# Attention's small matmuls: two places of a half step instead of four

## The chip, the cores and the metric

The kernel runs on one core of a Trainium2 chip. The metric is the device time of one execution in microseconds (us); lower is better. The engines named here are PE (TensorE, matmuls), DVE (VectorE), ACT (ScalarE), POOL (GpSimd) and SP, whose queue starts the transfers. Each engine takes its instructions in the order of the program and meets the others through semaphores.

## The reference, cut to what matters

One layer of an encoder, applied to two requests of 512 tokens each, so 1024 tokens. Cut to the attention branch:

```python
proj = rmsnorm(x) @ w_in                    # 1024 tokens x 1024, into q, k, v of 3 groups x 8 heads x 64
q, k = rope(rmsnorm(q)), rope(rmsnorm(k))   # per head
for g, (window, dilation) in enumerate(((128, 1), (512, 4), (2048, 16))):
    s = q @ k.T * 64 ** -0.5                # within the group's band
    p = exp(s - max(s)); o = p @ v          # sums and maxima are kept, the groups are joined later
```

Around it stand an RG-LRU branch, the output product and a convolutional FFN, which the change does not touch.

## The kernel before

**Stages.** The program runs through the norm and the recurrent branch (to about 410 us), the projections of v, k and q with the attention in between (410 to 975 us), the gate product `GELU(x @ w)` (to about 1080 us), the output product and the FFN. Every large product is split into three matmuls (high x high, high x low, low x high) of 128x512, lines L758 to L760 in the attention stage. I call these three, for one slice `k` of the contraction, a *slice*.

**The attention stage** is a loop over nine column blocks (`ci`: v, k, q of group 0, then of groups 1 and 2) and within it over eight token tiles `t`. One pass is a *step*: eight slices into one accumulator `ps`. A step is cut into two *half steps* of four slices (`hlf` 0 and 1), and between those slices the small matmuls of the attention of earlier tiles are put by hand:

- `slot_qk()` takes two *units* (512 score columns each) and issues their scores into `sp` (L642). On DVE it issues, per unit, mask add (L651), row maximum (L654) and a scaling of it (L656), then the exponentials on ACT (L658), which write `p`. In groups 1 and 2 it acts in every other half step.
- `slot_pt(new)` transposes the `p` of the two units that were scored a half step before: four transposes each into a PSUM tile `pt` (L666), and a copy to `pT` by DVE (L668).
- `slot_pv()` multiplies the transposed pairs with v into `o` (L679); ACT copies a finished `o` out (L682).
- `pend_T()` runs where a normed q or k tile is due (only in half step 0): four transposes of `kn` into a tile `pt` (L606), and a copy to `qkT` by DVE (L608). It also makes new units.

At the end of a q or k step `qk_norm` squares the finished `ps` on ACT (L577) and sums it on DVE (L580). A half step later DVE scales (L586, L588), and another one later it rotates (L595 to L597); the rotated `kn` is what `pend_T` transposes two steps after its product.

**The tile that both kinds of transposes share** has two buffers:

```python
pt = ps2.tile([128, 4, 128], F32, tag="tr", bufs=2, name="pt")   # in to_T (L606) and in emit_pt (L666)
```

A third tile of this tag may be written only when the copy out of the first is done. The other accumulators have three (`proj`), two (`s`) and one (`o`) bank.

**Order around the change.** In a half step: slice, `slot_qk`, slice, `slot_pv`, slice, (in half step 0) `pend_T`, slice, `slot_pt`, `tick`. `tick` lets the deferred scaling or rotation go to DVE. The gate stage goes on with the same slots until the units are used up, eight slices to a half step, with `pend_T` directly ahead of `slot_pt`.

Of the kernel before, what the change touches and what calls it, by code (L numbers as in the profile page):

```python
# [112 lines left out]
def layer_kernel(ctx: ExitStack, tc: tile.TileContext, xs_in, norm1_g, w_in, conv_w, conv_b, lru_wa, lru_ba,  # L113
# [518 lines left out]
    def emit_scores(us):  # L632
        for u in us:
            u.sp = ps2.tile([128, 512], F32, tag="s", bufs=2, name="sp")
        nk = len(us[0].keys)
        for i in range(len(us[0].heads)):
            for j in range(nk):
                c0 = (i * nk + j) * 128
                for u in us:
                    h, kk = u.heads[i], u.keys[j]  # L640
                    p0 = 64 * (h % 2)
                    PE.matmul(out=u.sp[:, c0:c0 + 128], lhsT=u.qT[p0:p0 + 64, h // 2, :],  # L642
                              rhs=kk[0][p0:p0 + 64, h // 2, :], start=True, stop=True)

    def emit_qk(u):
        sp, nh = u.sp, len(u.heads)
        if u.first:
            u.t.num = ap.tile([128, 528], F32, tag="num", bufs=2, name="num")
        h0 = u.heads[0]
        p = ap.tile([128, nh, u.w], F32, tag="p", bufs=4, name="p")  # L650
        V.tensor_tensor(out=p, in0=sp.rearrange("p (h k) -> p h k", h=nh),  # L651
                        in1=u.mask.rearrange("p (o k) -> p o k", o=1).to_broadcast([128, nh, u.w]), op=ALU.add)
        mx = u.t.num[:, 512 + h0:512 + h0 + 2 * nh - 1:2]
        V.tensor_reduce(out=mx, in_=p, axis=AX.X, op=ALU.max)  # L654
        nm = ap.tile([128, nh], F32, tag="nm", bufs=4, name="nm")
        V.tensor_scalar(out=nm, in0=mx, scalar1=-0.125, scalar2=None, op0=ALU.mult)  # L656
        for i in range(nh):
            act(out=p[:, i], in_=p[:, i], func=AF.Exp, scale=0.125, bias=nm[:, i:i + 1],  # L658
                accum_out=u.t.num[:, 520 + h0 + 2 * i:521 + h0 + 2 * i])
        u.p = p  # L660
# [11 lines left out]
    def emit_pv(u):  # L672
        tl = u.t
        if u.first:
            tl.o = ps2.tile([128, 512], F32, tag="o", bufs=1, name="o")
        nk = len(u.keys)
        for i, h in enumerate(u.heads):
            for j, kk in enumerate(u.keys):
                PE.matmul(out=tl.o[:, 64 * h:64 * h + 64], lhsT=u.pT[:, i * nk + j, :], rhs=kk[1][:, 64 * h:64 * h + 64],  # L679
                          start=(j == 0), stop=(j == nk - 1))  # L680
        if u.last:
            A.copy(out=tl.num[:, 0:512], in_=tl.o)  # L682
            dst = num_d[tl.g]
            if tl.g == 0:
                t0 = 64 + 128 * tl.qi
                if tl.qi < 7:
                    SP.dma_start(out=dst[t0:t0 + 128, :], in_=tl.num)
                else:
                    SP.dma_start(out=dst[T - 64:T, :], in_=tl.num[0:64])
                    SP.dma_start(out=dst[0:64, :], in_=tl.num[64:128])  # L690
            else:
                b, a = divmod(tl.qi, 4)
                SP.dma_start(out=dst[S * b:S * b + S, :].rearrange("(j a) c -> a j c", a=4)[a], in_=tl.num)
            ndone[tl.g, tl.qi] = True
# [5 lines left out]
    def slot_qk():  # L700

        turn[0] += 1
        if not units or (units[0].g and turn[0] % 2):
            return []
        new = [units.popleft(), units.popleft()]
        emit_scores(new)
        for u in new:
            emit_qk(u)
        return new

    def slot_pv():
        for u in infl2:
            emit_pv(u)
        infl2.clear()

    def slot_pt(new):
        for u in infl:
            emit_pt(u)
        infl2.extend(infl)
        infl.clear()  # L720
        infl.extend(new)
# [12 lines left out]
    def pend_T():  # L734
        while pend and pend[0][0] <= step[0]:
            _, kn, isq, gg, tt = pend.popleft()
            tT = to_T(kn, isq)
            if not isq:
                kt[gg, tt] = tT
            elif gg == 0:  # L740
                ks = [tt, (tt + 1) % 8]
                add_units(0, tt, tT, [(kt[0, x], vt[0, x]) for x in ks], masks["edge" if tt % 4 == 3 else "band"])
            else:
                add_units(gg, tt, tT, [(kt[gg, tt], vt[gg, tt])], masks[gg])

    for ci in range(9):
        g, typ = ci // 3, "vkq"[ci % 3]
        sl8 = ws.take(8)
        order = [7, 0, 1, 2, 3, 4, 5, 6] if (g == 0 and typ == "q") else list(range(8))
        for t in order:  # L750
            cols = lhs_cols(g, t, typ == "q")
            ps = ps2.tile([128, 512], F32, tag="proj", bufs=3, name="ps")
            ws.adv(1)
            for hlf in range(2):
                for k in range(4 * hlf, 4 * hlf + 4):
                    hi, lo = sl8[k]
                    a, b = xh[:, k, cols], xl[:, k, cols]
                    PE.matmul(out=ps, lhsT=a, rhs=hi, start=(k == 0), stop=False)  # L758
                    PE.matmul(out=ps, lhsT=a, rhs=lo, start=False, stop=False)  # L759
                    PE.matmul(out=ps, lhsT=b, rhs=hi, start=False, stop=(k == KD - 1))  # L760
                    if ci == 8 and t == order[-1]:
                        ws.done("a", 1)
                        ws.adv(1)
                    if k % 4 == 0:
                        new = slot_qk()
                    if k % 4 == 1:
                        slot_pv()
                    if k == 2:
                        pend_T()
                slot_pt(new)  # L770
                tick()
            if typ == "v":
                v_t = ap.tile([128, 512], F32, tag="v", bufs=8, name="v_t")
                A.copy(out=v_t, in_=ps)
                vt[g, t] = v_t
            else:
                if g == 0:
                    ri = (4 if typ == "q" else 0) + t % 4
                else:
                    ri = 8 + t % 4  # L780
                kn = qk_norm(ps, g if typ == "q" else 3 + g, ri, typ == "q")
                pend.append((step[0] + 2, kn, typ == "q", g, t))
            step[0] += 1
        if ci < 8:
            ws.done("ab"[ci % 2], 8)
# [71 lines left out]
    for c in range(KR):  # L857
        if c == ATT_DONE:
            assert not (units or infl or infl2 or pend)
            close(cm_a)  # L860
            cm_y, yp = open_pool("y", side="right")
            cm_o, op_ = open_pool("oT", side="right")
            new_oT()
            for cc in list(held):
                y_split(cc, held.pop(cc))
        slabs = ws.take(2)
        for b in range(2):
            ps = ps2.tile([128, 512], F32, tag="proj", bufs=3, name="ps")
            sl = slice(S * b, S * b + S)
            for ks in (range(1), range(1, 3), range(3, 8)):  # L870
                mm3(ps, wcol(slabs, 0), wcol(slabs, 1), lambda k: xh[:, k, sl], lambda k: xl[:, k, sl], KD, ks)
                if ks[0] == 0:
                    new = slot_qk()
                elif ks[0] == 1:
                    slot_pv()
            if b == 0:
                pend_T()
            slot_pt(new)
            if b == 1:
                ws.done("a", 2)  # L880
                if c + 1 < KR:
                    h_load(c + 1)
                if c >= 2:
                    cg = comb_load(c - 2)
                    defer(3, lambda t=c - 2, cg=cg: combine(t, cg))
            tick()
            ws.adv(1)
            hT = hts.pop((c, b))
            if b == 0 and c < ATT_DONE:
                gl = p3.tile([128, S], F32, tag="yhold", bufs=ATT_DONE, name="yhold")  # L890
            else:
                gl = p3.tile([128, S], F32, tag="gl", bufs=2, name="gl")
            act(out=gl, in_=ps, func=AF.Gelu_apprx_tanh)
            V.tensor_tensor(out=gl, in0=hT, in1=gl, op=ALU.mult)
            if b == 1:
                defer(1, lambda c=c, gl=gl: SP.dma_start(out=y_d[128 * c:128 * c + 128, :], in_=gl))
            elif c < ATT_DONE:
                held[c] = gl
            else:
                y_split(c, gl)  # L900
        step[0] += 1
# [269 lines left out]
```

## Time and profile before

| | |
|---|---|
| time, median of 3 runs | 2167.48 us (2165.16 to 2169.90) |
| the profiled execution | 2167.51 us, its span 2165.7 us |
| PE busy | 2108.1 us, 97% of the span |
| DVE busy | 1072.7 us, 50% |
| ACT busy | 756.6 us, 35% |

PE's busy time contains modelled ends, so it says that PE rarely stands, not that it runs at its peak. What a move of matmuls costs is therefore read from the distance between starts. DVE's mean hides that its share differs by stage.

### The profile page before, as it was taken

Reading aid. Unit: us, or ns where it says so; the run is one execution under the profiler, and the core shown is the slowest. Engines: PE = TensorE matmul, PEld = TensorE weight load, DVE = VectorE, ACT = ScalarE, POOL = GpSimd, SP = SyncE. Lnnn points to the kernel's source line nnn. Section 1 sums busy time; section 2 is a strip of 40 time slices with the busy share of each in tenths; the row PEclk is TensorE's granted clock in tenths of the full one; section 3 lists DMA queues with packets and bytes.
Section 4 is the critical chain, followed back from the end, with each engine's and each line's share of the span. In section 5 each row is a group of like instructions: output and inputs, shape, how many; then the busy total and the mean of one; then the engine's idle time right before and its main releaser. Section 6 shows DMA issues by size and latency. Waiting matters only on the chain. (4 is left out here: it accounts for less than half of the span.)

```text
span 2165.7 us, 25959 instructions
## 1 busy us (share of the span) xinstructions
PE 2108.1 (97%) x9859; PEld 1756.0 (81%) x9859; DVE 1072.7 (50%) x1513; ACT 756.6 (35%) x1269; POOL 771.1 (36%) x658
## 2 busy tenths in 40 slices
PE   7999898999999999999999999999999999999999
PEld 5767676787899999998778888888888888888887
DVE  5499998427862671674654442333233332233324
ACT  4388787412431242145433432411221122212120
POOL 4345656634213422422445444421222222222220
PEclk9999999999999999999999999999999999999999
DMA  4534444411111111104555454211111111111112
GB/s 143 150 95 138 127 124 122 149 48 42 40 41 44 40 55 49 30 28 146 161 197 181 135 159 152 64 49 39 49 49 49 49 44 55 49 49 39 56 41 83
DMA packets 190299, 181.98 MB, mean 84 GB/s; under 512 B 27708, under 2 KB 142942, under 8 KB 190174
## 3 DMA queue, kind: packets, MB, share of 16 engines
q1 hardware_dynamic: 188126, 175.08, 26.6%
q0 software_dynamic: 2048, 5.25, 1.0%
q8 instruction: 78, 1.28, 0.3%
q14 instruction: 47, 0.39, 0.1%
HBM read 141.80 MB, written 33.23 MB: 81 GB/s over the span
## 5 line engine op out<-in xcount | busy, mean ns | idle before, releaser
L228 POOL TENSOR_TENSOR lo<-raw,hi 128x512 fp32r<-128x512 f32 (+1 forms) x384 | 508.8, 1337 | 881.9 <-ACT hi L227 839.1
L150 PE MATMUL ps<-x2h,lo 128*128 128x512 f32 x768 | 301.4, 392 | 0.0
L148 PE MATMUL ps<-x2h,hi 128*128 128x512 f32 x768 | 301.3, 392 | 0.0
L149 PE MATMUL ps<-x2l,hi 128*128 128x512 f32 x768 | 301.2, 392 | 0.0
L227 ACT CAST hi<-raw 128x512 fp32r<-128x512 f32 (+1 forms) x324 | 189.9, 605 | 305.3 <-issue 121.8
L758 PE MATMUL ps<-hi,xh 128*128 128x512 f32 x576 | 251.8, 437 | 0.0
L759 PE MATMUL ps<-lo,xh 128*128 128x512 f32 x576 | 229.1, 398 | 1.7 <-POOL lo L228 1.7
L1094 DVE TENSOR_TENSOR acc<-acc,psd 128x512 f32<-128x512 f32 x192 | 132.0, 687 | 199.3 <-PE psd L1093 199.3
L760 PE MATMUL ps<-hi,xl 128*128 128x512 f32 x576 | 228.6, 397 | 0.0
L148 PE MATMUL ps<-xh,hi 128*128 128x512 f32 x544 | 218.3, 401 | 4.3 <-DVE xc L354 4.3
L150 PE MATMUL ps<-xh,lo 128*128 128x512 f32 x544 | 217.1, 399 | 2.2 <-POOL lo L228 2.2
L149 PE MATMUL ps<-xl,hi 128*128 128x512 f32 x544 | 216.8, 399 | 0.0
L149 PEld LDWEIGHTS ps<-x2l,hi 128*128 128x128 f32 x768 | 144.2, 188 | 32.7
L148 PEld LDWEIGHTS ps<-x2h,hi 128*128 128x128 f32 x768 | 144.2, 188 | 32.5
L150 PEld LDWEIGHTS ps<-x2h,lo 128*128 128x128 f32 x768 | 144.2, 188 | 32.5
L759 PEld LDWEIGHTS ps<-lo,xh 128*128 128x128 f32 x576 | 157.4, 273 | 8.9 <-POOL lo L228 2.6
L758 PEld LDWEIGHTS ps<-hi,xh 128*128 128x128 f32 x576 | 155.2, 270 | 10.5 <-POOL hi L225 0.5
L760 PEld LDWEIGHTS ps<-hi,xl 128*128 128x128 f32 x576 | 155.3, 270 | 8.2
L1091 PE MATMUL psd<-hi,hh 128*128 128x512 f32 x384 | 151.6, 395 | 0.0
L1092 PE MATMUL psd<-lo,hh 128*128 128x512 f32 x384 | 151.5, 395 | 0.0
L1093 PE MATMUL psd<-hi,hl 128*128 128x512 f32 x384 | 151.5, 395 | 0.0
L1049 DVE SCALAR_TENSOR_TENSOR gc<-ps,vff,gc 128x1022 f32<-128x1022 f32 x24 | 30.8, 1281 | 229.2 <-ACT gc L1048 229.2
(188 smaller groups left out, 3540.5 us busy)
## 6 DMA issues: line engine op xcount, KB each, us to landing
raw<-in_w_in_dram SPq DMA_DIRECT2D x144, 256.0 KB
raw<-in_w_up_dram SPq DMA_DIRECT2D x96, 256.0 KB
raw<-in_w_down_dram SPq DMA_DIRECT2D x48, 256.0 KB
sg_d<-sgt SPq DMA_DIRECT2D x16, 512.0 KB
raw<-in_w_lru_out_dram SPq DMA_DIRECT2D x32, 256.0 KB
raw<-in_w_o_dram SPq DMA_DIRECT2D x32, 256.0 KB
cg<-num_d SPq DMA_DIRECT2D x24, 264.0 KB
num_d<-num SPq DMA_DIRECT2D x23, 264.0 KB
```

The source lines that it names most:

```text
L148: PE.matmul(out=ps, lhsT=a, rhs=b, start=(k == 0), stop=False)
L149: PE.matmul(out=ps, lhsT=a, rhs=rl(k), start=False, stop=False)
L150: PE.matmul(out=ps, lhsT=wl(k), rhs=b, start=False, stop=(k == n - 1))
L227: A.copy(out=hi[:, 0:n], in_=r[:, 0:n])
L228: G.tensor_tensor(out=lo[:, 0:n], in0=r[:, 0:n], in1=hi[:, 0:n], op=ALU.subtract)
L758: PE.matmul(out=ps, lhsT=a, rhs=hi, start=(k == 0), stop=False)
L759: PE.matmul(out=ps, lhsT=a, rhs=lo, start=False, stop=False)
L760: PE.matmul(out=ps, lhsT=b, rhs=hi, start=False, stop=(k == KD - 1))
L1091: PE.matmul(out=ps, lhsT=a[0][:, tl], rhs=w[0], start=(i == 0), stop=False)
L1092: PE.matmul(out=ps, lhsT=a[0][:, tl], rhs=w[1], start=False, stop=False)
L1093: PE.matmul(out=ps, lhsT=a[1][:, tl], rhs=w[0], start=False, stop=(i == 1))
L1094: V.tensor_tensor(out=acc[t][:, cl], in0=acc[t][:, cl], in1=ps, op=ALU.add)
```

## The change

The scores and value products of a half step are issued together, ahead of its first slice, value products first. The transposes of `kn` and of `p` are issued together behind the first slice (in the gate stage behind the second), so the remaining slices follow them. The number of instructions on PE and DVE is the same.

```diff
             for hlf in range(2):
+                slot_pv()
+                new = slot_qk()
                 for k in range(4 * hlf, 4 * hlf + 4):
                     hi, lo = sl8[k]
                     a, b = xh[:, k, cols], xl[:, k, cols]
...
                     if ci == 8 and t == order[-1]:
                         ws.done("a", 1)
                         ws.adv(1)
+                    if k == 0:
+                        pend_T()
                     if k % 4 == 0:
-                        new = slot_qk()
-                    if k % 4 == 1:
-                        slot_pv()
-                    if k == 2:
-                        pend_T()
-                slot_pt(new)
+                        slot_pt(new)
                 tick()
...
             ps = ps2.tile([128, 512], F32, tag="proj", bufs=3, name="ps")
             sl = slice(S * b, S * b + S)
-            for ks in (range(1), range(1, 3), range(3, 8)):
+            slot_pv()
+            new = slot_qk()
+            for ks in (range(2), range(2, 8)):
                 mm3(ps, wcol(slabs, 0), wcol(slabs, 1), lambda k: xh[:, k, sl], lambda k: xl[:, k, sl], KD, ks)
                 if ks[0] == 0:
-                    new = slot_qk()
-                elif ks[0] == 1:
-                    slot_pv()
-            if b == 0:
-                pend_T()
-            slot_pt(new)
+                    if b == 0:
+                        pend_T()
+                    slot_pt(new)
```

On PE, in the q steps of group 1, before: from the pending transposes in half step 0 to the value products in half step 1 there is a slice between any two kinds.

```order
L606 MATMUL pt<-ident,kn 128x128 x4
L758 MATMUL ps<-hi,xh 128x512
L759 MATMUL ps<-lo,xh 128x512
L760 MATMUL ps<-hi,xl 128x512
L666 MATMUL pt<-ident,p 128x128 x8
...
L642 MATMUL sp<-qkT 128x128 x8
...
L679 MATMUL o<-v_t,pT 128x64 x8
```

The same place of the changed kernel, where the lines of a slice have moved by two (L760 to L762). Now the eight transposes of `p` follow the four of `kn` at once, and nine large matmuls follow both:

```order
L606 MATMUL pt<-ident,kn 128x128 x4
L666 MATMUL pt<-ident,p 128x128 x8
L760 MATMUL ps<-hi,xh 128x512
...
L679 MATMUL o<-v_t,pT 128x64 x8
L642 MATMUL sp<-qkT 128x128 x8
L760 MATMUL ps<-hi,xh 128x512
```

The scores have moved behind the value products, and both stand ahead of the four slices of the half step.

The same transposes with what they wait for, changed kernel. The rows are the end of the four of `kn`, the four of the first unit and the four of the second:

```order
L606 MATMUL pt<-ident,kn 128x128 x3
L666 MATMUL pt<-ident,p 128x128 [waits PE_49,Activation_49]
L666 MATMUL pt<-ident,p 128x128 [waits Activation_49] x3
L666 MATMUL pt<-ident,p 128x128 [waits DVE_49,Activation_49]
L666 MATMUL pt<-ident,p 128x128 [waits Activation_49] x3
```

The first transpose of the second unit waits for DVE: its tile is the buffer that the pending transposes filled just before.

On DVE the order is the same before and after. In a half step 0 of group 0 it is this, with the copy of the pending transposes (L608) behind the six operations of the scores:

```order
L651 TENSOR_TENSOR p<-sp,msk 128x512
L654 TENSOR_REDUCE num<-p 128x2
L656 TENSOR_SCALAR nm<-num 128x2
L651 TENSOR_TENSOR p<-sp,msk 128x512
L654 TENSOR_REDUCE num<-p 128x2
L656 TENSOR_SCALAR nm<-num 128x2
L608 COPY qkT<-pt 128x512
L668 COPY pT<-pt 128x512 x2
```

Nothing moved in these rows; what moved is when PE wants their results.

## Rows read from the trace of the kernel before

**Rows 1.** The page: busy time, share of the span and instructions of each engine.
```profile
PE 2108.1 (97%) x9859; PEld 1756.0 (81%) x9859; DVE 1072.7 (50%) x1513; ACT 756.6 (35%) x1269; POOL 771.1 (36%) x658
```

**Rows 2.** Busy time by stretch: length, PE, PEld, DVE, ACT, POOL, clock, DMA share, GB/s.
```profile
524.00:646.00 122.00, 119.70 (x889) 105.54 (x888) 93.28 (x177) 47.41 (x154) 25.36 (x24) 1.00 0.13 37
```

**Rows 3.** Timeline of PE, first pair of group 1: start, length, instruction.
```profile
738.49 1.16 PE L642 MATMUL sp<-qkT 64*128 64x128 f32 x16
739.58 0.62 PE L758 MATMUL ps<-hi,xh 128*128 128x512 f32 x1
...
744.07 0.60 PE L606 MATMUL pt<-ident,kn 128*128 128x128 f32 x4
744.42 0.60 PE L758 MATMUL ps<-hi,xh 128*128 128x512 f32 x1
744.86 0.40 PE L759 MATMUL ps<-lo,xh 128*128 128x512 f32 x1
...
745.33 0.60 PE L666 MATMUL pt<-ident,p 128*128 128x128 f32 x4
746.48 0.63 PE L666 MATMUL pt<-ident,p 128*128 128x128 f32 x4 [0.55 <-DVE qkT L608]
746.86 0.60 PE L758 MATMUL ps<-hi,xh 128*128 128x512 f32 x1
```

**Rows 4.** Timeline of PE, the next step of group 1.
```profile
749.88 1.89 PE L679 MATMUL o<-v_t,pT 128*128 128x64 f32 x16
751.58 0.61 PE L758 MATMUL ps<-hi,xh 128*128 128x512 f32 x1
```

**Rows 5.** Timeline of DVE, first pair of group 1.
```profile
739.68 0.69 DVE L651 TENSOR_TENSOR p<-sp,msk 128x512 f32<-128x512 f32 x1
...
743.37 0.29 DVE L597 TENSOR_TENSOR kn<-kn,rt 128x128 f32<-128x128 f32 x1
745.05 0.69 DVE L580 TENSOR_REDUCE ss<-sq 128x8 f32<-128x512 f32 x1 [1.39 <-ACT sq L577]
745.65 0.68 DVE L608 COPY qkT<-pt 128x512 f32<-128x512 f32 x1
```

**Rows 6.** Timeline of ACT, first pair of group 1: last exponential, then the square.
```profile
744.35 0.19 ACT L658 ACTIVATION_READ_ACCUMULATOR p<-p,nm 128x1 f32 x1
744.44 0.57 ACT L577 ACTIVATE sq<-ps 128x512 f32<-128x512 f32 x1
```

**Rows 7.** Timeline of PE, first pair of group 0.
```profile
534.15 0.60 PE L666 MATMUL pt<-ident,p 128*128 128x128 f32 x4
537.05 0.63 PE L666 MATMUL pt<-ident,p 128*128 128x128 f32 x4 [2.30 <-ACT p L658]
537.43 0.48 PE L758 MATMUL ps<-hi,xh 128*128 128x512 f32 x1
537.75 0.39 PE L759 MATMUL ps<-lo,xh 128*128 128x512 f32 x1
537.98 0.40 PE L760 MATMUL ps<-hi,xl 128*128 128x512 f32 x1
```

**Rows 8.** Timeline of all engines, the same place: DVE alone.
```profile
532.96 0.68 DVE L651 TENSOR_TENSOR p<-sp,msk 128x512 f32<-128x512 f32 x1
...
536.22 0.68 DVE L608 COPY qkT<-pt 128x512 f32<-128x512 f32 x1
```

**Rows 9.** Timeline of all engines, gate stage: the transposes of `p`.
```profile
983.52 0.63 PE L666 MATMUL pt<-ident,p 128*128 128x128 f32 x4 [0.86 <-DVE qkT L608]
```

**Rows 10.** Busy time by stretch, columns as in rows 2 (clock third from the end).
```profile
537.90:541.30 3.40, 3.40 (x33) 2.78 (x31) 3.30 (x7) 0.00 (x0) 0.00 (x0) 1.00 0.16 59
...
1139.91:1143.32 3.41, 3.41 (x9) 2.64 (x8) 1.12 (x1) 1.64 (x3) 3.18 (x3) 0.50 0.40 119
1143.32:1146.73 3.41, 3.41 (x16) 2.81 (x15) 1.93 (x3) 0.40 (x1) 0.79 (x2) 1.00 0.89 256
```

**Rows 11.** Timeline of PE, the last wait ahead of the fall in rows 10.
```profile
1138.46 0.47 PE L148 MATMUL ps<-yh,hi 128*128 128x512 f32 x1 [2.37 <-DVE thb L948]
```

## The prediction

> **What bounds the kernel now.** I read four views. The page first: PE is busy for 97% of the span, DVE for half of it [rows 1], so PE's stream of matmuls sets the time, and anything that makes PE stand in the attention stage is paid in full. Then the busy time by stretch, since DVE's half is a mean: while group 0's attention runs, DVE works 93.28 of 122 us [rows 2]. There DVE is nearly as full as PE, and a wait of PE for something at the end of DVE's queue is not short. Third, PE's timeline, read by starts, since the lengths overlap. Last, the timelines of DVE and ACT beside it, to see what the transposes wait for.
>
> **What the change takes away: borders.** It adds and removes no instruction, it moves them. Each return from small to large matmuls costs something: the first large one is followed by the next after 0.44 us where its weights are read strided (744.42 to 744.86) [rows 3], after 0.32 where they are not (537.43 to 537.75), against 0.23 in the stream (537.75 to 537.98) [rows 7]. So a merged border gives back 0.21 in groups 1 and 2 and 0.09 in most of group 0. A group 0 step has seven groups of small matmuls and keeps four (3 x 0.09 = 0.27); a step of groups 1 and 2 has four and keeps two (0.42). Over about 8 steps of group 0, three of them strided, and 16 of the others: 5 x 0.27 + 3 x 0.63 + 16 x 0.42 = 10 us. This is the whole gain in sight, and it is netted below. What the passage from value products to scores costs has no row. From below it is nothing; from above I take another border, 0.09 to 0.21 on some 30 places, 3 to 6 us. I take it near nothing, since both sides are small matmuls, and leave the rest to the range.
>
> **What it adds: a wait in the middle of a half step.** Three tiles of the tag `tr` are now written in a row: pending, first unit, second unit. There are two buffers, so the second unit's four transposes wait until DVE has copied the pending tile (L608). The order shows that wait. Behind it on PE stand the three remaining slices, nine large matmuls, and with them the end of the half step and all that follows. Before the change L608 had a slice and most of a half step more to be done.
>
> *Groups 1 and 2.* The first pair of group 1 shows the whole chain in the kernel before, because it already waits there. Scores start at 738.49, DVE takes them up at 739.68 [rows 3, 5]; the exponentials end at 744.5 and only then ACT squares the finished `ps`, at 744.44 [rows 6]; DVE sums it at 745.05 and copies the pending tile at 745.65 [rows 5]; the second four transposes start at 746.48 [rows 3]. From scores to there it is 7.99 us, and no link of it is a large matmul, so it does not shrink when PE's order changes.
> When will PE want these four? After the change, counted from the start of the scores: 1.09 for the scores (738.49 to 739.58). Then the four slices of half step 1: 18 large ones take 4.49 (739.58 to 744.07), of which the first 0.44, so 0.238 each, and twelve take 3.06. Then one slice of half step 0, 0.71; the pending transposes 0.35 (744.07 to 744.42); the first unit's four, 0.38 (as 746.48 to 746.86) [rows 3]. Together 5.59. The wait is 7.99 - 5.59 = 2.40 us. Less the borders, a step grows by 2.40 - 0.42 = 1.98. Value products (1.70, 749.88 to 751.58) [rows 4] stand before the scores in both counts and drop out.
> The pair of q tile t meets the pending tile of t + 1, and the square is in the chain while q steps last: in group 1 for six pairs, in group 2 for five in the loop (the sixth falls into the gate stage). The first pair of each group waits 0.55 already and merges one border: +1.4. Group 1: 5 x 1.98 + 1.4 = 11.3. Group 2: 4 x 1.98 + 1.4 = 9.3.
>
> *Group 0* has scores in every half step, so L608 stands behind the six operations of scores issued just before. Mask add to L608 takes 3.26 (532.96 to 536.22) [rows 8], L608 to the second four 0.83 (to 537.05) [rows 7]; with 1.19 from scores to mask add that is 5.28. PE wants them after 1.09 + 0.79 (a slice behind small ones, 0.32 + 2 x 0.23) + 0.35 + 0.38 = 2.61. The wait is 2.67, less 0.27 of borders 2.4 a step. Of seven such half steps the first already waits 2.30 [rows 7]; there the chain starts a slice earlier (0.8) and three slices (2.2) move behind it: +1.4. Four cost 2.4; the last two run in strided steps, where the slice is longer and the borders save more: 1.8 each. Group 0: 1.4 + 9.6 + 3.6 = 14.6.
>
> *The rest.* In the gate stage both kinds already stand side by side and wait 0.86 [rows 9]; with pairs that have no square in the chain, and the last ones without pending tiles, which keep the borders' gain, I put -1 in all. The transfers of a step move with it, on DMA engines that are busy to 0.13 in that stretch [rows 2], and no instruction of SP or POOL is passed.
>
> The waits' sum is 14.6 + 11.3 + 9.3 - 1 = 34 us.
>
> **The clock.** A wait of PE can also cost afterwards. After the wait of 2.37 us at 1138 [rows 11] the granted clock went to 0.50 (1.2 GHz) for 3.41 us, in which 9 large matmuls started, against 16 in the 3.42 us behind it at 1.00 (2.4 GHz) [rows 10]: seven lost, at 0.23 to 0.24 some 1.65 us. After the wait of 2.30 in group 0 [rows 7] the clock stayed at 1.00 [rows 10]. These two lie closest together; longer waits in the trace were followed by a fall, shorter ones not. My new waits, counted as the profile counts them (less 0.22 for the modelled end of four transposes, 0.60 against 0.38), are 2.4 to 2.5 in four or five half steps of group 0 and about 2.2 in the thirteen others, where part of it is moved ahead of the pending transposes, which wait for the rotation (743.37) [rows 5]. They straddle the border. I take six falls of 1.65: 10 us; the bounds are none and all eighteen, 0 and 30.
> The Trainium skill, "TensorE: Matmul & The Clock Gate", section "PE-mode transpose", says that transposes do not count as PE work for the clock in the way that matmuls do. By that rule the whole stretch from pending transposes to the last four would be rest, and all eighteen would end in a fall. This trace does not bear it out: the first pair of group 0 has just such a stretch and kept its clock.
>
> **Sum.** The profiled execution took 2167.51, the median of the runs is 2167.48, so they need no shift: 2167.5 + 34 + 10 = 2211.5, **2211 us**.
>
> **The rivals.** *Falls after every wait:* 2167.5 + 34 + 30 = 2231. For it, twelve transposes and the wait make some 3.5 us without a large matmul; against it, the same pair of group 0. 0.15.
> *Half the wait:* one of the two kinds of chain is shorter than in its model place, for instance because in groups 1 and 2 the square finds ACT free: 2167.5 + 14 to 20, with up to three falls, 2180 to 2193. For it, one pair per kind is all that shows the chain; against it, its links are single operations that stand in order on DVE and ACT. 0.13.
> *Faster:* the copy L608 is done when PE comes to the second unit, and only the borders' 10 us count: 2157. The place is that one wait; it decides when it falls below 0.42 us in groups 1 and 2 and 0.27 in group 0, so L608 would have to start 2 us earlier than the rows have it. For it, in later steps of the kernel before L608 is in time. Against it, a slice stood between. 0.04.
> *No change:* waits that are as large as the borders, within 0.2%, which is 4 us and about what runs of this kernel can tell apart: 0.04.
> My forecast, 2203 to 2221, has 0.64.
>
> **How the numbers follow.** Faster 0.05, same 0.04, slower 0.91. The range runs from the upper end of the half wait to the case of all falls: 2193 to 2232. It leaves out most of the half wait, the two small cases and a tail above, about 0.2.
>
> **What would show it.** Right: in q steps of each group the second four L666 wait 2 to 2.7 us, put down to qkT L608, seven times in group 0 and about six in each other group; these steps last 2 us longer; L679 goes over into L642 without a gap; the granted clock falls some times between 530 and 1020 us, where before it was 1.00; the stages before 410 us and behind the gate stage keep their length. Wrong: L608 earlier than in the rows (scores taken up sooner, squares ahead of exponentials); long waits at L679 for pT, which I count at nothing because the copies are due 0.1 us before PE wants them in group 0 and over 1 us before in the others; or falls after all waits or none.

## The result: 2.8% slower, and the profile after

The changed kernel takes 2228.76 us (median of four runs, 2227.56 to 2230.16) against 2167.25 us before (four runs, 2165.16 to 2169.90): ratio 1.0283, interval 1.0266 to 1.0301. The forecast was 2211 us within 2193 to 2232. The profiled execution took 2227.56 us with a span of 2225.8 us, 60.1 us more than before.

I cut both traces into stages by the starts of the large matmuls, 24 to a step. The gate stage is counted here from its first large matmul to the first transpose of the joined attention output. Lengths in us; the last column adds up the prediction's terms without its clock term.

| stage | before | after | more | predicted |
|---|---|---|---|---|
| start to the third q step of group 0, where its first pairs come due | 522.3 | 523.2 | +0.9 | 0 |
| group 0 with its pairs (10 steps) | 127.8 | 149.6 | +21.8 | +14.6 |
| 14 steps without pairs | 84.2 | 84.1 | -0.1 | 0 |
| group 1 (10 steps) | 96.4 | 113.8 | +17.4 | +11.3 |
| 14 steps without pairs | 84.2 | 84.2 | 0.0 | 0 |
| group 2 in the loop (6 steps) | 61.1 | 70.6 | +9.5 | +9.3 |
| gate stage | 63.8 | 73.9 | +10.1 | -1 |
| what follows | 1125.9 | 1126.3 | +0.4 | 0 |

All of the loss lies where pairs are in flight. The page shows no more work: the counts are those of [rows 1], and the busy time of PE grew by 17 us in a span that grew by 60. The page after:

```profile
PE 2124.7 (95%) x9859; PEld 1767.9 (79%) x9859; DVE 1071.2 (48%) x1513; ACT 758.3 (34%) x1269; POOL 770.9 (35%) x658
```

The waits of PE (total in us, count, longest) name the tile that both kinds of transposes share. Before, the first two rows held 2.7 us in four waits and 2.3 us in one.

```profile
PE pt L666 <- DVE qkT L608: 27.5, 14, 7.1
PE pt L666 <- ACT p L658: 19.5, 7, 4.3
PE pt L606 <- DVE kn L597: 4.2, 12, 0.9
```

**A pair of group 1**, timeline of PE (start, length, instruction, idle time before it and what ended it), answering to [rows 3]:

```profile
825.90 1.89 PE L679 MATMUL o<-v_t,pT 128*128 128x64 f32 x16
827.72 1.16 PE L642 MATMUL sp<-qkT 64*128 64x128 f32 x16
828.81 0.62 PE L760 MATMUL ps<-hi,xh 128*128 128x512 f32 x1
...
833.04 0.63 PE L606 MATMUL pt<-ident,kn 128*128 128x128 f32 x4 [0.30 <-DVE kn L597]
833.50 0.60 PE L666 MATMUL pt<-ident,p 128*128 128x128 f32 x4
835.75 0.63 PE L666 MATMUL pt<-ident,p 128*128 128x128 f32 x4 [1.65 <-DVE qkT L608]
836.13 0.60 PE L760 MATMUL ps<-hi,xh 128*128 128x512 f32 x1
...
838.45 0.33 PE L679 MATMUL o<-v_t,pT 128*128 128x64 f32 x2
```

DVE at the same place, answering to [rows 5]:

```profile
828.91 0.69 DVE L651 TENSOR_TENSOR p<-sp,msk 128x512 f32<-128x512 f32 x1 [2.65 <-PE sp L642]
...
834.32 0.69 DVE L580 TENSOR_REDUCE ss<-sq 128x8 f32<-128x512 f32 x1 [1.43 <-ACT sq L577]
834.92 0.68 DVE L608 COPY qkT<-pt 128x512 f32<-128x512 f32 x1
```

From the scores to the second four transposes it is 827.72 to 835.75, 8.03 us; the model pair gave 7.99. The second four start 2.25 us after the first four, of which 0.38 is work: 1.87 of standing, and 0.30 ahead of the pending transposes. The passages between two kinds of small matmuls are not free: from the value products to the scores it is 1.82 (825.90 to 827.72) where the same products took 1.70 ahead of a slice [rows 4], and from the pending transposes to those of `p` 0.46 (833.04 to 833.50) where it was 0.35 to the next slice [rows 3].

**A half step 0 of group 0**, timeline of PE, answering to [rows 7]:

```profile
586.75 1.16 PE L642 MATMUL sp<-qkT 64*128 64x128 f32 x16
...
588.64 0.60 PE L606 MATMUL pt<-ident,kn 128*128 128x128 f32 x4
589.08 0.60 PE L666 MATMUL pt<-ident,p 128*128 128x128 f32 x4
592.33 0.63 PE L666 MATMUL pt<-ident,p 128*128 128x128 f32 x4 [2.65 <-ACT p L658]
592.72 0.48 PE L760 MATMUL ps<-hi,xh 128*128 128x512 f32 x1
```

DVE there, answering to [rows 8]:

```profile
587.95 0.69 DVE L651 TENSOR_TENSOR p<-sp,msk 128x512 f32<-128x512 f32 x1 [1.13 <-PE sp L642]
...
589.39 0.68 DVE L656 TENSOR_SCALAR nm<-num 128x2 f32<-128x2 f32 x1
589.99 0.68 DVE L651 TENSOR_TENSOR p<-sp,msk 128x512 f32<-128x512 f32 x1
...
591.43 0.17 DVE L656 TENSOR_SCALAR nm<-num 128x2 f32<-128x2 f32 x1
591.50 0.69 DVE L608 COPY qkT<-pt 128x512 f32<-128x512 f32 x1
```

DVE works there without a gap, and L608 is the seventh operation after the scores. PE's row names the exponentials (L658) as releaser, but L608 starts 0.83 us ahead of the second four, as in [rows 7, 8]. Which of the two it was is tested below.

**The gate stage**, timeline of PE and of ACT, answering to [rows 9]:

```profile
1027.34 0.60 PE L666 MATMUL pt<-ident,p 128*128 128x128 f32 x4
1035.00 1.08 PE L666 MATMUL pt<-ident,p 128*128 128x128 f32 x4 [7.05 <-DVE qkT L608]
```
```profile
1027.49 1.64 ACT L227 CAST hi<-raw 128x512 fp32r<-128x512 f32 x3
1032.42 0.62 ACT L227 CAST hi<-raw 128x512 fp32r<-128x512 f32 x1 [3.29 <-DMA raw<-in_w_in_dram]
1032.94 0.59 ACT L577 ACTIVATE sq<-ps 128x512 f32<-128x512 f32 x1
```

Here the square of the last q tile stands on ACT behind four weight casts (L227), the last of which waits 3.29 us for its transfer. The row sum and L608 wait for the square, and PE for L608.

**The clock.** Between 523 us and the end of the gate stage the granted clock was 1.00 throughout before. After, it falls to 0.50 (1.2 GHz for 2.4) seven times: at 536, 557, 768, 796, 809, 1031 and 1055 us. The falls at 536 and 1031 last 6.83 us, the others 3.41. Busy time by stretch, columns as in rows 2; the second to fourth row are the wait of one pair of group 1 and what follows it:

```profile
524.00:646.00 122.00, 102.51 (x736) 88.54 (x734) 84.69 (x160) 41.55 (x133) 22.72 (x22) 0.96 0.11 32
792.90:795.66 2.76, 1.11 (x11) 0.90 (x9) 1.88 (x3) 1.32 (x4) 1.06 (x2) 1.00 0.00 0
795.66:799.07 3.41, 3.41 (x10) 2.76 (x9) 2.36 (x3) 0.00 (x0) 2.02 (x2) 0.50 0.15 19
799.07:802.48 3.41, 3.41 (x35) 3.13 (x34) 0.12 (x1) 0.58 (x1) 0.00 (x0) 1.00 0.17 62
```

The timeline of PE there gives the price of one fall:

```profile
795.56 0.80 PE L760 MATMUL ps<-hi,xh 128*128 128x512 f32 x1
...
799.35 0.89 PE L679 MATMUL o<-v_t,pT 128*128 128x64 f32 x7
```

The nine large matmuls behind the second four take 3.79 us (795.56 to 799.35) in this step and 2.32 (836.13 to 838.45) in the step shown above: 1.47 lost. Seven at this price are 10 us, an estimate: the two long falls lie partly in the wait itself.

### The profile page after: what moved, and what is told of

Its sections match the earlier page's. It is cut to its first block, busy times and chain, and to the rows that moved or that the text cites. A ratio compares the mean times of both kernels' runs of the same rounds, so it can differ in the third digit from the quotient of the medians.

```text
span 2225.8 us, 25964 instructions
## 1 busy us (share of the span) xinstructions
PE 2124.7 (95%) x9859; PEld 1767.9 (79%) x9859; DVE 1071.2 (48%) x1513; ACT 758.3 (34%) x1269; POOL 770.9 (35%) x658
## 5 line engine op out<-in xcount | busy, mean ns | idle before, releaser
L228 POOL TENSOR_TENSOR lo<-raw,hi 128x512 fp32r<-128x512 f32 (+1 forms) x384 | 509.4, 1338 | 903.1 <-ACT hi L227 855.6
L227 ACT CAST hi<-raw 128x512 fp32r<-128x512 f32 (+1 forms) x324 | 189.7, 605 | 311.7 <-issue 121.8
L760 PE MATMUL ps<-hi,xh 128*128 128x512 f32 x576 | 247.6, 430 | 0.0
L762 PE MATMUL ps<-hi,xl 128*128 128x512 f32 x576 | 231.1, 401 | 0.0
L760 PEld LDWEIGHTS ps<-hi,xh 128*128 128x128 f32 x576 | 156.2, 271 | 11.8 <-POOL hi L225 0.5
L762 PEld LDWEIGHTS ps<-hi,xl 128*128 128x128 f32 x576 | 156.5, 272 | 9.2
```

Of the source, the lines that this page charges most:

```text
L227: A.copy(out=hi[:, 0:n], in_=r[:, 0:n])
L228: G.tensor_tensor(out=lo[:, 0:n], in0=r[:, 0:n], in1=hi[:, 0:n], op=ALU.subtract)
```

## Experiments

In the diffs, lines with a minus are those of the kernel that each starts from. Times are medians, ratios against the kernel before, run beside it on the same chip, with 95% intervals. A wait in brackets is the profile's; counted by starts (from the first to the second four transposes of `p`, less their 0.38 us of work) the same wait is 0.22 longer.

**1. A third buffer for the shared tile** (from the changed kernel; a `proj` bank is given up for it). The same at every other place of the two tags.

```diff
-pt = ps2.tile([128, 4, 128], F32, tag="tr", bufs=2, name="pt")
+pt = ps2.tile([128, 4, 128], F32, tag="tr", bufs=3, name="pt")
...
-ps = ps2.tile([128, 512], F32, tag="proj", bufs=3, name="ps")
+ps = ps2.tile([128, 512], F32, tag="proj", bufs=2, name="ps")
```

> The changed kernel, with three buffers instead of two for the tile of both kinds of transposes, and two instead of three for the accumulator of the projections (PSUM has no bank left). Theory: the second unit's transposes wait because their buffer is still to be copied out by DVE. Then with a third buffer those waits go, with them the falls of the clock behind them, and the borders' gain is seen: 2157 to 2175 us, waits of L666 for qkT L608 near zero. Rival: the waits come from the exponentials or from DVE being late as such; then the second unit waits as long as before and the time stays within 10 us of 2229.

Measured 2181.31 us, 1.0061 [1.0044, 1.0078], 47 us less than the changed kernel. Group 0 lasts 133.5 us, group 1 98.1, group 2 61.5, the gate stage 69.3. No row for L666 is left among the long waits of PE, and others are in their place:

```profile
PE o L679 <- DVE pT L668: 8.7, 7, 3.2
PE pt L606 <- DVE kn L597: 4.5, 13, 0.9
```

So the shared buffer is the cause of most of the loss, all seven waits put down to L658 among them. It came out 6 us above the upper end of what I expected. In group 0 the value products now wait five times, 0.46 to 0.74 us, and 2.3 us at the first pair, for the copies L668, which stand at the end of the same row of DVE work. The seventh of these waits, the longest, lies in the gate stage, where the granted clock then shows 0.50 for 10.2 us; that stage keeps 69.3 us where experiment 2 has 63.1. The third buffer moves part of the wait one step on.

**2. The same banks in the kernel before**, to see that the trade of banks is not itself the gain.

> The kernel before with the same trade of banks (three for the transposes, two for the projections). It shows what the trade does by itself. Theory: the kernel before waits for that buffer at three or four places only (2.3, 0.6, 0.9 and about 0.9 us), so 2160 to 2167 us if two accumulators suffice. Rival: two accumulators are too few, and each step waits for the scaling of the one two steps back: over 2180 us.

Measured 2163.78 us, 0.9984 [0.9975, 0.9993]. The banks alone are worth 3 to 4 us, so at equal banks the new order still costs 17.5 us (2181.31 - 2163.78): some 7 us in group 0, 6 in the gate stage, and most of the rest in groups 1 and 2.

**3 and 4. The two halves of the change.** Third: the new order in the loop, the gate stage as before. Fourth: the reverse, with this edit alone.

```diff
-            for ks in (range(1), range(1, 3), range(3, 8)):
+            slot_pv()
+            new = slot_qk()
+            for ks in (range(2), range(2, 8)):
...
-            if b == 0:
-                pend_T()
-            slot_pt(new)
+                if ks[0] == 0:
+                    if b == 0:
+                        pend_T()
+                    slot_pt(new)
```

> The changed order in the loop over the nine column blocks, the old order in the gate stage. Theory: in the gate stage the changed order waits 7.9 us for a square that stands on ACT behind the splits of the gate's first weights, and 2.5 us in the next tile; with the old order there these waits fall back to about 1 us each, together with two or three falls of the clock: 2217 to 2222 us. Rival: the wait belongs to the loop's changed order and only shows in the gate stage: 2226 us or more.

> The old order in the loop, the changed order in the gate stage. Theory: the gate stage alone costs 7 to 11 us: 2174 to 2179 us, with one wait of 6 to 8 us at the first pair of transposes of the gate stage. Rival: with the loop's old order everything reaches the gate stage in time, and it costs nothing: 2165 to 2169 us.

Measured: the loop alone 2219.64 us, 1.0236 [1.0221, 1.0252]; the gate stage alone 2176.08, 1.0038 [1.0023, 1.0053]. Together 52.7 + 9.2 = 61.9 us over the kernel before, and the whole change 61.5. The waits of the fourth kernel (total, count, longest):

```profile
PE pt L666 <- DVE qkT L608: 7.4, 4, 4.3
```

Two of the four, 4.27 and 2.06 us, are the gate stage's own; I had expected one of 6 to 8. In the third kernel the gate stage waits 2.67 and 0.44 us where I expected about 1 each, and lasts 66.7 us against 63.8 before. So the times came as expected, but a part of the gate stage's loss comes in with the loop's order.

**5. Pending transposes ahead of the scores**, with the transposes of `p` where the change puts them. L608 is then wanted a slice and the scores later, and on DVE it stands ahead of the mask adds.

```diff
                 slot_pv()
+                if hlf == 0:
+                    pend_T()
                 new = slot_qk()
...
-                    if k == 0:
-                        pend_T()
```

> The changed kernel, with the pending transposes moved between the value products and the scores (in the loop alone), so that on DVE their copy L608 stands ahead of the six operations of the scores, not behind them. Theory: in group 0 the wait comes from that place in DVE's queue, so its seven waits of about 3 us go; DVE's copies of the pairs are as late as with the third buffer, so some waits of value products come in their place. In groups 1 and 2 the copy still stands behind the norm's row sum, and their waits stay. 2207 to 2215 us, group 0 some 16 us shorter, group 1 within 2 us of the changed kernel. Rival: in group 0 the second unit waits for its exponentials (the profile puts seven waits down to L658); then its waits stay and the time is over 2222 us.

Measured 2214.39 us, 1.0211 [1.0197, 1.0225]. Group 0 shrinks from 149.6 to 130.8 us; as its first scores now stand a half step earlier, it is fairer to count it with the step before, 155.6 to 139.7. Timeline of PE, at the place shown for the changed kernel:

```profile
586.46 0.60 PE L606 MATMUL pt<-ident,kn 128*128 128x128 f32 x4
...
587.85 1.16 PE L642 MATMUL sp<-qkT 64*128 64x128 f32 x16 [0.79 <-DVE qkT L608]
...
589.74 1.04 PE L666 MATMUL pt<-ident,p 128*128 128x128 f32 x8
```

All eight transposes of `p` run in one stretch, with nothing changed in the exponentials. With experiment 1 this settles that the row "ACT p L658" named the wrong releaser. In groups 1 and 2 the order helps less, 109.3 us in group 1, and steps without pairs grow (86.0 us for 84.1 in each stretch of 14), because the pending transposes now come earlier than their input is rotated:

```profile
PE pt L666 <- DVE qkT L608: 18.0, 13, 7.1
PE pt L606 <- DVE kn L597: 16.0, 19, 1.4
```

**6. Transposes of `p` two slices later** (`k % 4 == 2`), pending ones unmoved. L608 gets two slices of cover.

```diff
-                    if k % 4 == 0:
+                    if k % 4 == 2:
                         slot_pt(new)
```

> The changed kernel, with the transposes of the pairs behind the third slice of a half step instead of the first (in the loop alone). Theory: the moment at which the buffer comes free is set by DVE and ACT and does not move, PE wants it two slices (1.4 us) later, so each of some 17 waits shrinks by 1.4 us and most of the clock's falls go: 2190 to 2204 us, waits about 1.7 us in group 0 and 1 us in groups 1 and 2. Rival: DVE's chain moves with the transposes, waits stay as long and only shift: over 2220 us.

Measured 2194.45 us, 1.0120 [1.0106, 1.0134]. Group 1 falls to 100.2 us with 0.34 to 0.40 left of its 1.87 (I had expected 1), group 0 to 136.1, and no fall of the clock is left in the loop. The gate stage, which was not edited, keeps its 74.4 us. The waits:

```profile
PE pt L666 <- ACT p L658: 9.5, 7, 2.9
PE pt L666 <- DVE qkT L608: 9.4, 2, 7.4
```

**7. Both kinds side by side, but at the end of the half step** (from the kernel before, the loop alone): adjacency with the whole cover behind the scores.

```diff
-                    if k == 2:
+                    if k == 3:
                         pend_T()
                 slot_pt(new)
```

> The kernel before, with the pending transposes moved behind the fourth slice, so that both kinds stand together at the end of the half step (in the loop alone); scores and value products as before. Theory: standing together costs by itself about the copy of DVE and its signals less the first unit's four transposes, 0.5 to 0.9 us in some 19 half steps, and gives back a border (0.09 to 0.21): 2172 to 2181 us. It is far less than the changed kernel's 61 us, of which most comes from standing together early, while DVE still works on the scores or waits for the norm. Rival: standing together is the whole cost wherever it is: over 2195 us.

Measured 2177.05 us, 1.0043 [1.0029, 1.0056], 9.2 us over the kernel before. Timeline of PE, a pair of group 1:

```profile
772.77 0.63 PE L666 MATMUL pt<-ident,p 128*128 128x128 f32 x4 [0.44 <-DVE qkT L608]
```

Standing side by side makes a wait of 0.65 us by starts, and the steps grow by 0.50 to 0.63. Of the loop's 52.7 us these 9.2 are less than a fifth; the rest comes with the place early in the half step.

**8. The row sum behind the copies** (from the changed kernel): L580 and the two small POOL operations are issued after the copies of `slot_pt`, to see whether square and sum are a link of the chain in groups 1 and 2.

```diff
-        V.tensor_reduce(out=ss, in_=sq..., axis=AX.X, op=ALU.add)
-        G.tensor_scalar(out=ss, ...)
-        G.tensor_tensor(out=rs, ...)
+        late.append(sums)     # the same three, issued at the end of slot_pt
```

> The changed kernel, with the norm's row sum on DVE (and the two POOL operations behind it) issued behind the copies of the transposes of the next half step instead of ahead of them. Theory: in groups 1 and 2 the copy L608 waits for exponentials, then the square, then this sum; without it L608 follows the rotation, and the second unit waits for the last exponentials alone, 1.1 to 1.2 us instead of 2.0: 11 times some 0.9 to 1.2 us and up to three falls of the clock, 2208 to 2219 us; group 0 within 3 us of the changed kernel. The gate stage's wait of 7 us, which is the same sum behind the gate's weight splits, goes too, which would bring 2202 to 2212 us. Rival: the sum is not in the chain: 2224 us or more.

Measured 2220.65 us, 1.0241 [1.0227, 1.0256]: between the expectation and its rival. The link is there. The row for the second four in group 1 (L672 in this kernel) has lost 1.2 us of its wait:

```profile
798.20 0.63 PE L672 MATMUL pt<-ident,p 128*128 128x128 f32 x4 [0.44 <-DVE qkT L614]
```

Group 1 lasts 105.1 us for 113.8 and group 2 66.0 for 70.6. But scaling and rotation wait for the sums, so the next pending transposes are late (L612 here), and the steps without pairs grow by 2.7 and 3.1 us:

```profile
PE pt L612 <- DVE kn L603: 13.1, 24, 2.0
```

In the gate stage the first wait is gone as well (0.44), but the second grew from 2.06 to 4.87. The edit pays with one wait for the other and does not measure the chain's price alone.

**9. Weight casts behind the square** (from the changed kernel): the four casts of the loop's last half step are issued after the last square.

```diff
-                    if ci == 8 and t == order[-1]:
+                    if ci == 8 and t == order[-1] and hlf == 0:
                         ws.done("a", 1)
                         ws.adv(1)
...
                 pend.append((step[0] + 2, kn, typ == "q", g, t))
+                if ci == 8 and t == order[-1]:
+                    for _ in range(4):
+                        ws.done("a", 1)
+                        ws.adv(1)
```

> The changed kernel, with four of the eight weight splits of the loop's last step (those of its second half step) issued behind the square of the norm instead of ahead of it. Theory: the 7.1 us wait at the first pair of the gate stage is that square, which stands on ACT behind those four splits; then the wait falls to 1.5 to 2.5 us, the second (2.3 us) stays: 2221 to 2225 us. Rival: the splits are late for another reason (their transfers) and the first gate slices wait for them as long as the transposes did: 2227 us or more.

Measured 2224.57 us, 1.0267 [1.0252, 1.0283]. Of the wait of 7.05 us 1.60 are left, and the square starts behind the last exponential, as the timelines of PE and of ACT show:

```profile
1030.47 0.63 PE L666 MATMUL pt<-ident,p 128*128 128x128 f32 x4 [1.60 <-DVE qkT L608]
```
```profile
1028.43 0.57 ACT L577 ACTIVATE sq<-ps 128x512 f32<-128x512 f32 x1
```

What I didn't expect is that the gate stage shrank by only 2.2 us, to 71.7, still 7.9 above the kernel before: its second wait grew from 2.06 to 4.87. There L608 stands on DVE behind the gate's own product, and the product of the half step before (the first row) waits 8.44 us for its transfer, with the mask adds behind it:

```profile
1041.97 0.69 DVE L896 TENSOR_TENSOR yhold<-hT,yhold 128x512 f32<-128x512 f32 x1 [8.44 <-DMA hT<-h_d]
...
1051.19 0.69 DVE L896 TENSOR_TENSOR gl<-hT,gl 128x512 f32<-128x512 f32 x1 [4.64 <-ACT gl L895]
1051.80 0.69 DVE L608 COPY qkT<-pt 128x512 f32<-128x512 f32 x1
```

In the changed kernel that product started at 1041.87, no later. So PE, no longer held up by the first wait, comes to the second one earlier, and what the second waits for is not earlier by as much. The casts are the cause of the first wait, not of the gate stage's whole loss.

**10. Scores and value products together, without the rest** (from the kernel before): the other part of the change, but with the value products behind the scores and both behind the first slice. The gate stage gets the same edit.

```diff
                     if k % 4 == 0:
                         new = slot_qk()
-                    if k % 4 == 1:
                         slot_pv()
```

> The kernel before (two buffers, three accumulators) with scores and value products together behind the first slice, and nothing else of the change. Theory: it gains what the same step gained with three buffers, 2 to 4 us (2163 to 2166 us), since neither kind of transposes moves. Rival: with two buffers value products wait: 2168 us or more.

Measured 2167.54 us, 1.0000 [0.9991, 1.0008]. The three attention stages are 1.5 us shorter in its trace, all in all no change of time that can be told apart. A merged border gave 0.10 to 0.13 us in nearly every paired step of groups 1 and 2, and 0.02 in most steps of group 0, which merge two; in one step of group 0 a new wait for L608 took back 0.48. My 2 to 4 us were not confirmed.

**11. The same with three buffers** (experiment 2 with that edit).

> The kernel before with three buffers for the transposes and two for the projections, and with one part of the change alone: value products right behind the scores after the first slice; both kinds of transposes at their old places. Theory: one border less in about 30 half steps, 0.09 to 0.21 us each, less what passing from scores to value products costs: 2159 to 2163.5 us. Rival: value products, a slice earlier, wait for DVE's copies of the pairs in group 0: 2165 us or more.

Measured 2160.84 us, 0.9967 [0.9955, 0.9980], the fastest here, ahead of both kernels. The stages are 0.5, 0.8 and 0.5 us shorter than in experiment 2, 1.8 in all where experiment 10 has 1.5. Whether the pairing gains more with three buffers than with two I can't settle from medians some 2 us apart.

## Why the prediction was right, and what it mis-sized

**The wait for L608: right, in place and in cause.** Experiment 1 takes away the sharing and with it three quarters of the loss; experiment 6 gives cover back and the wait shrinks with it. In groups 1 and 2 the waits were 1.6 us on the profile, shorter than the 2 to 2.7 given as a sign.

**Groups 1 and 2: right in the chain, in the sum by some luck.** The chain of 7.99 us measured 8.03. A step was to grow by 1.98, and those without a fall grew by 1.94 to 2.06, the first pair of group 2 by 1.46 for 1.4. But PE stands 2.17 (1.87 and 0.30) and not 2.40, since it comes to these transposes 0.27 later than reckoned, and the borders give back some 0.14 and not 0.42; that the two errors cancel is luck. Group 2 grew by 9.5 where 9.3 was forecast. Group 1's 17.4 hold three falls (4.4 at 1.47), which leaves 13.0 against 11.3; 1.4 of the difference lies in its last two steps, which the sum left out. That the square and the sum are links is shown by experiment 8.

**Group 0: right in kind, 4 us too small.** 21.8 less two falls (2.9) is 18.9, forecast 14.6. From scores to the second four it takes 5.58 us (586.75 to 592.33), forecast 5.28. The missing 0.3 is on DVE: mask add to L608 takes 3.55 (587.95 to 591.50) where [rows 8] gave 3.26, as the two L656 take 0.68 and 0.17 where they took 0.17 and 0.39 in the model place. PE comes 0.1 later (from the pending transposes to the first of `p` it is 0.44, 588.64 to 589.08, for 0.35), so it stands 2.87 for 2.67. Steps without a fall grew by 2.9 to 3.0 where 2.4 was forecast: the 0.27 of borders is not there either. With the last two steps this makes some 2.8 of the 4.3. The other 1.5 lie at the first pair, whose fall lasts 6.83 us and is counted here at the price of one of 3.41; I didn't separate them further.

**The borders: 10 us of gain that hardly showed, a term that failed.** The prediction took the passage between two kinds of small matmuls near nothing. It measures 0.12 from value products to scores and 0.09 to 0.11 from the pending transposes to those of `p`, as much as a border of 0.09 gives back and half of one of 0.21. Experiment 10 merges one border of each half step and gains 1.5 us in the trace's attention stages and nothing in the time.

**The gate stage, "I put -1 in all": the step that failed.** It came to +10.1, some 7 without the falls. I took it that both kinds already stood side by side there and waited 0.86 [rows 9], and overlooked that they stood behind eight slices, and after the change behind two. With the cover gone, a queue on ACT that had not mattered, the casts and their transfer ahead of the last square, set the first wait. Experiment 4 shows the place (+9.2 us), experiment 9 the casts as cause of the first wait; with most of that wait gone the stage is still 7.9 us longer than before, and its second wait stands behind DVE's gate products; what each of their links costs stays open.

**The clock: right in size, by luck.** Six falls at 1.65 were forecast, seven came at some 1.47. They lie differently than I thought: two of the seven waits in group 0, three of the six in group 1, though these are shorter than the 2.30 that kept its clock in [rows 7], none of the five of the same length in group 2, two in the gate stage. The Trainium skill, "TensorE: Matmul & The Clock Gate", section "PE-mode transpose", says that transposes do not count as PE work for the clock in the same way. As the prediction put that rule, each of the eighteen stretches would end in a fall; 13 of them kept the clock at 1.00.

**Sum.** 44 us were forecast, 60.1 came. The difference of 16.1 is the gate stage (10.1 + 1 - 2.9 = 8.2), group 0 (4.3), group 1 (1.7), group 2 (0.2), the falls (0.3) and the stages outside (1.2), up to rounding. The time measured lies above the 2203 to 2221 of the forecast proper: the room up to 2232 was made for falls after every wait, and the gate stage and group 0 filled it. That the range held is in part luck.

**The rivals.** "Half the wait", "faster" and "no change" fall with the chain's 8.03 us and the time. "Falls after every wait" gave 2231, near the time measured, but by a mechanism that the trace refutes: seven falls, not eighteen.

## What to carry to other kernels

Where two kinds of work share a rotating buffer, count how many tiles of it are written between two returns of the engine that empties it: a third tile in two buffers turns an order that looks tidier into a wait. For each moved step, count at every place in the program, the last stage too, how much independent work stood between a result and its use before, and how much stands there now. The cover of eight slices in the gate stage hid a queue that the waits before showed as 0.86 us. And before counting on a merged border, measure the passage that it leaves: here it took as much as half of the border or all of it.

## What the runs showed of the hardware that I had not expected

**A small DVE operation can end with a POOL operation beside it, up to 0.5 us late.** L656 on 128x2 elements takes 0.17 us alone and 0.68 beside this row of POOL's timeline of the changed kernel:

```profile
588.78 1.27 POOL L228 TENSOR_TENSOR lo<-raw,hi 128x512 fp32r<-128x512 f32 x1
```

Both end at about 590.06. It is no accident of one row: all seven L656 that run beside an L228 in this trace take 0.30 to 0.68 us and end within 0.03 us of it, as do the seven of the kernel before, and the 57 with no long POOL operation beside them take 0.17. L654 with its 128x512 elements, which runs beside the same POOL row, takes its usual 0.69. The Trainium skill, "SBUF — State Buffer", section "SBUF: two separate sides", says that GpSimd and a DVE operation in a two-port mode, or with two inputs from SBUF, shut each other out of a shared pair of ports for a whole instruction. The rows of L656 agree with it; no run here shows which mode L656 is in or takes the POOL operation away.

**Waits of the same length do not all end in a fall of the clock.** In group 1 the six waits are 1.59 to 1.65 us by the profile and three were followed by 0.50. What tells them apart stays open.
